# Splitting B22 alone, and T1 and t2 as one operation, in the 7-product steps of a transformer block

## The chip, the cores and the metric

The kernel runs on one core of a Trainium2 chip. The metric is the device time of one execution in microseconds (us); the time before is the median of three runs. A core has five engines with a queue of instructions each: TensorE (PE, with its weight loads shown apart as PEld), VectorE (DVE), ScalarE (ACT), GpSimd (POOL) and SyncE (SP). Each works through its queue in order; semaphores make one wait for another.

## The reference

One layer of a residual block on x of 256 tokens by 4096 channels in float32. Cut to what matters here:

```python
h = rms_norm(x, pre_norm_gain)
proj = h @ w_in                       # 4096 x 24704, split into q, k, v, gates, ...
y_a = dsa_attention(q, k, v, ...) * silu(gate_a)
y_b = ssd_mixer(xs, z, bm, cm, ...)
merged = sigmoid(g0) * (y_a @ w_branch_attn) + sigmoid(g1) * (y_b @ w_branch_ssd)
x = x + rms_norm(merged @ w_out, post_norm_gain)
```

Nearly all the work is in products of a 256-row activation with large float32 weights.

## The kernel before

**Number format.** Every float32 operand is split into a high half h (rounded by a copy to TensorE's fp32r format on ScalarE) and a low half l (operand minus h, on VectorE). A product is three matmuls: al·bh, ah·bl, ah·bh, each 128x128 by 128x512.

**Pairs.** A pair of 512-column blocks of a weight matrix is one call of `pair_gemm`. It runs over 16 (or 8) steps; a step has 256 rows of the weight, loaded by SP as two tiles, `ra` (B12 and B22) and `rb` (B11 and B21), two steps ahead. The four 128x512 blocks meet four 128x128 blocks of the activation. A step of kind "S" uses a Strassen-Winograd scheme of 7 products (21 matmuls), one of kind "D" or "R" the plain 8 products (24 matmuls). There are 226 S steps. The list of S steps in a pair is a tuple such as `SX` = (1, 3, 4, 6, 7, 9, 10, 12, 14); `SG`, used from the fourth of the eight gate pairs on, ends in 12, 13, 14 (in the last gate pair the steps from 8 on are plain). The activation's sums S1 to S4 are made beforehand (`ext`, against `b` for the plain blocks).

**An S step.** POOL issues a DMA that adds B11 onto B12 in `ra[:, 0]`, which makes T1's source. Then the weight's halves are made, for products in this order: with B21 (bank 2) and B11 (1), with B22 (3), with T1 (5), t2 (6), t3 (7) and t4 (4). In the code before: `rb` is split whole (1024 columns); B22 is copied to h (L636) and subtracted to l (L637); T1's source is copied to h (L638); t2 = T1 - B22 is formed in place over B22 (L641); t3 and t4 = `rb` - t2 are formed in place (L642, 1024 columns); T1's low half is made (L644, kept in this place by `keep_in_program_order`); t2 is split alone, then t3 and t4 together. L641 and L642 are called the block sums below.

**Tiles.** The halves lie in tiles `wh` and `wl` of 1024 columns from a ring of 4 each, and in one half tile (`wh1`, `wl1`, 512 columns, a single buffer), which t2 uses. A tile is free again when TensorE has done the last matmul that reads it.

**Order.** The order of each engine's instructions is set by a scheduler when the kernel is built. It walks the program by priority and takes what is ready by its own estimates, so that work of other parts (evictions of a pair's banks L563 to L590, the rotation of q and k L739 to L744, attention, the convolution L887) is put in between, and matmuls of a product can be moved by a place or two.

Of the kernel before, what the change touches and what calls it, by code (L numbers as in the profile page):

```python
# [13 lines left out]
AF = mybir.ActivationFunctionType  # L14
# [34 lines left out]
def fused_block(tc, x, xT, w_qi, w_misc, w_q0, w_qk, w_vg, w_x, w_z, w_gate, w_br, w_out2,  # L49
                percol, rows, tabs, tris, pgain, out):  # L50
    nc = tc.nc
    V, A, G, T = nc.vector, nc.scalar, nc.gpsimd, nc.tensor
# [21 lines left out]
    def fbit(ap):  # L74
        return ap.bitcast(F32)
# [427 lines left out]
    def split_tiles(n):  # L503
        if n == 1:
            return (whp.tile([P, 1, NW], F32R, tag="wh1", bufs=1, name="wh"),
                    wlp.tile([P, 1, NW], F32R, tag="wl1", bufs=1, name="wl"))
        return (whp.tile([P, n, NW], F32R, tag="wh", name="wh"),
                wlp.tile([P, n, NW], F32R, tag="wl", name="wl"))

    def split(src, n, sign=1, at=None):  # L510
        h, l = at() if at else split_tiles(n)
        A.activation(h, src, AF.Copy, scale=float(sign))  # L512
        if sign < 0:
            V.scalar_tensor_tensor(l, src, -1.0, fbit(h), ALU.mult, ALU.subtract)  # L514
        else:
            V.tensor_sub(l, src, fbit(h))  # L516
        return [(h[:, j, :], l[:, j, :]) for j in range(n)]
# [23 lines left out]
    def pair_gemm(what, mode, chunk, plan, outs, evac, hooks={}, pace=1, tail=0, spares=None, done=None):  # L541

        while len(live) > 1:
            drain(live.popleft())
        left = {}
        for _, kind in plan:
            for j, n in USES[kind].items():
                left[j] = left.get(j, 0) + n
        ps = {}
        dest = []  # L550

        def product(j, i, name, w):
            (ah, al), (bh, bl) = form(i, name), w
            first = j not in ps
            if first:
                ps[j] = bank(phys[j])
            left[j] -= 1
            for n, (l, r) in enumerate(((al, bh), (ah, bl), (ah, bh))):
                T.matmul(ps[j], l, r, start=first and n == 0, stop=left[j] == 0 and n == 2)  # L559

        def early():
            dest.extend(outs())
            A.activation(dest[0], ps[1], AF.Copy)  # L563
            V.tensor_add(dest[1], ps[6], dest[0])
            V.tensor_add(dest[2], ps[7], dest[1])

        def late():
            if not dest:
                dest.extend(outs())
                A.activation(dest[1], ps[5], AF.Copy, scale=-1.0)  # L570
                return
            V.tensor_add(dest[1], ps[5], dest[1])
            if 8 in ended:
                V.tensor_sub(dest[3], dest[3], ps[5])
                return
            V.scalar_tensor_tensor(dest[3], ps[5], -1.0, dest[2], ALU.mult, ALU.subtract)

        def rest():
            c11, c12, c21, c22 = dest
            if 1 not in ps:  # L580
                A.activation(c11, ps[2], AF.Copy)
                A.activation(c21, ps[4], AF.Copy)
                V.tensor_sub(c22, c12, ps[8])
                V.tensor_sub(c12, c12, ps[3])
                return
            V.scalar_tensor_tensor(c12, ps[3], -1.0, c12, ALU.mult, ALU.subtract)
            if 8 in ps and 8 not in ended:
                V.tensor_sub(c22, c22, ps[8])
            V.tensor_add(c11, ps[2], c11)
            V.tensor_add(c21, ps[4], c21)  # L590

        def end():
            rest()
            live.append(push(evac(dest)))

        def closing(tails):
            c11, c12, c21, c22 = dest
            V.scalar_tensor_tensor(c12, ps[3], -1.0, c12, ALU.mult, ALU.subtract)
            V.tensor_add(c11, ps[2], c11)
            done(0, dest)  # L600
            for j in (8, 4):
                for i, w in tails:
                    for k in (1, 2):
                        product(j, i, f"A2{k}", w[k, 2 if j == 8 else 1])
            V.tensor_sub(c22, c22, ps[8])
            V.tensor_add(c21, ps[4], c21)
            done(1, dest)

        tails = []
        after = max([n for n, (_, kind) in enumerate(plan) if kind == "S"], default=-2) + 1  # L610
        ended = []
        loaded = deque()

        def fetch(n):
            i, kind = plan[n]
            ra, rb = raw_tile(), raw_tile()
            load_half(ra, chunk(i), 0)
            load_half(rb, chunk(i), 1)
            if kind == "S":
                nc.gpsimd.dma_start(ra[:, 0, :], chunk(i)[:, HK, :], accum_op=ALU.add)  # L620
            loaded.append((ra, rb))

        for n in range(LEAD):
            fetch(n)
        for n, (i, kind) in enumerate(plan):
            if n + LEAD < len(plan):
                fetch(n + LEAD)
            ra, rb = loaded.popleft()
            if n in hooks:
                hooks[n]()  # L630
            assert kind_of[i] == what, (n, i, kind_of, len(aux))
            assert kind == "R" or ext_n[i] == {"S": 4, "D": 2}[kind], (n, i, ext_n)
            if kind == "S":
                b11, b21 = split(rb, 2)
                h, l = split_tiles(2)
                A.activation(h[:, 1, :], ra[:, 1, :], AF.Copy)  # L636
                V.tensor_sub(l[:, 1, :], ra[:, 1, :], fbit(h[:, 1, :]))  # L637
                A.activation(h[:, 0, :], ra[:, 0, :], AF.Copy)  # L638
                if n == 1:
                    run_pending()  # L640
                V.tensor_sub(ra[:, 1, :], ra[:, 0, :], ra[:, 1, :])  # L641
                V.tensor_sub(rb, rb, ra[:, 1:2, :].to_broadcast([P, 2, NW]))  # L642
                tc.keep_in_program_order(
                    V.tensor_sub(l[:, 0, :], ra[:, 0, :], fbit(h[:, 0, :])))  # L644
                t1, b22 = ((h[:, j, :], l[:, j, :]) for j in range(2))
                t2, = split(ra[:, 1:2, :], 1)
                t3, t4 = split(rb, 2)
                now = {1: ("A11", b11), 2: ("A12", b21), 3: ("S4", b22), 4: ("A22", t4),
                       5: ("S1", t1), 6: ("S2", t2), 7: ("S3", t3)}
                for j in (2, 1, 3, 5, 6, 7, 4):  # L650
                    product(j, i, *now[j])
            else:
                w = {}
                at = spares if n == len(plan) - tail + 1 else None
                w[1, 2], w[2, 2] = split(ra, 2, -1, at)
                w[1, 1], w[2, 1] = split(rb, 2, 1, at)
                if n == 0 and len(pending) > 1 and turned[0] == "aux":
                    pending.pop(0)()
                if n == 1:
                    run_pending()  # L660
                if n >= len(plan) - tail:
                    assert kind == "R" and dest
                    tails.append((i, w))
                    for k, j in ((1, 3), (2, 3), (1, 2), (2, 2)):
                        product(j, i, f"A1{k}", w[k, 1 if j == 2 else 2])
                    step(2 * pace)
                    continue
                if n == after:
                    early()
                    if not left.get(5):  # L670
                        late()
                        ended.append(5)
                if n == len(plan) - 1 and dest and not ended and left.get(8) == 0:
                    V.scalar_tensor_tensor(dest[3], dest[2], -1.0, ps[8], ALU.mult, ALU.subtract)
                    ended.append(8)
                todo = [(k, j) for j in ((5, 3, 2, 4) if kind == "D" else (3, 8, 2, 4))
                        for k in (1, 2)]
                for k, j in todo:
                    name = {2: f"A1{k}", 4: f"A2{k}", 8: f"A2{k}", 5: f"A2{k}",
                            3: f"D{k}" if kind == "D" else f"A1{k}"}[j]  # L680
                    product(j, i, name, w[k, 1 if j in (2, 4) else 2])
                    if (k, j) == todo[3]:
                        step(pace)
            step(pace)
        if tail:
            closing(tails)
            return
        if 5 not in ended:
            pending.append(late)
        pending.append(end)  # L690
        turn(mode)
# [733 lines left out]
```

## Time and profile before

| what | value |
|---|---|
| time, median of 3 runs (lowest, highest) | 2805.91 us (2803.67, 2806.32) |
| profiled execution | 2806.09 us |
| its span, first to last instruction | 2804.2 us |
| mean granted TensorE clock | 0.998 |
| PE / DVE / ACT / POOL busy | 99% / 90% / 65% / 8% |
| DMA | 651.75 MB, mean 232 GB/s |

The page gives the busy time of each engine, then 40 slices of the span, the DMA queues, the chain of waits that ended last, and groups of instructions by line. On the chain, 93% of the span is PE and 4% DVE. A row of a group reads: line, engine, operation, written tile <- read tiles, shapes and count, then busy us and mean ns of one, then the engine's idle time just before them and what ended it. A row of the timeline reads: start, duration, engine, line, operation, tiles, count of merged instructions, and in brackets the idle time before it and what ended it.

### The profile page before, as it was taken

The page shows a single profiled execution, that of the slowest core. Times are in us where ns is not written, and L with a number is a line of the kernel's source. Part 1 is how long each engine was busy: PE and PEld are TensorE (multiplying, and loading weights), DVE is VectorE, ACT ScalarE, POOL GpSimd, SP SyncE. Part 2 cuts the span into 40 slices and gives each one's busy share as a digit, 9 for nine tenths or more (in the row PEclk, how much of TensorE's full clock was granted, in tenths as well). Part 3 has the DMA queues.
Part 4 walks back from the last instruction along what each step waited for, and adds up shares of the span by engine and source line. Part 5 has one row for each costly group of instructions (what it writes and reads, how often), then busy time and mean ns, then how long its engine had stood idle before and what let it go on. Part 6 is the DMA issues. An engine that isn't in the chain of part 4 may idle for free.

```text
span 2804.2 us, 36892 instructions
## 1 busy us (share of the span) xinstructions
PE 2780.0 (99%) x12598; PEld 2282.7 (81%) x12598; DVE 2536.2 (90%) x3352; ACT 1815.1 (65%) x2564; POOL 226.6 (8%) x271
## 2 busy tenths in 40 slices
PE   9999999999999999999999999999999999999998
PEld 7877888888888888787888788888888888788886
DVE  7668999999999988989898999999987999988998
ACT  7444566665666666887788866666665656656664
POOL 0100000000000000000000010111010100000000
PEclk9999999999999999999999999999999999999999
DMA  9544777777777777576767788888877788867886
GB/s 379 194 165 143 221 222 230 236 211 221 232 227 229 220 220 233 173 226 200 220 190 217 224 255 255 254 253 251 262 260 246 249 274 265 276 223 234 241 253 214
DMA packets 205326, 651.75 MB, mean 232 GB/s; under 512 B 23120, under 2 KB 23888, under 8 KB 205136
## 3 DMA queue, kind: packets, MB, share of 16 engines
q1 hardware_dynamic: 161424, 566.52, 60.1%
q0 software_dynamic: 34784, 66.60, 13.5%
q10 hardware_dynamic: 8928, 16.26, 1.5%
q8 instruction: 99, 1.62, 0.2%
q14 instruction: 91, 0.75, 0.1%
HBM read 629.37 MB, written 19.92 MB: 232 GB/s over the span
## 4 chain that ended last, share of the span: by engine, by line
PE 93%; DVE 4%; ACT 1%; issue 1%; DMA 1%; DVEq 0%; SPq 0%; ACTq 0%
PE p L559 80%; PE p L211 3%; PE p L212 3%; PE p L213 3%; PE p L382 1%; DVE wl L516 1%; ACT wh L512 0%; PE p L413 0%; PE p L951 0%; DVE raw L642 0%; PE p L816 0%; PE p L783 0%; DVE cacc L887 0%; DVE raw L641 0%; ACT L889 0%
## 5 line engine op out<-in xcount | busy, mean ns | idle before, releaser
L559 PE MATMUL p<-wh,b 128*128 128x512 f32 x4536 | 1490.3, 393 | 0.4 <-ACT wh L512 0.2
L512 ACT ACTIVATE wh<-raw 128x1024 fp32r<-128x1024 f32 (+1 forms) x1154 | 1093.8, 972 | 612.3 <-DVE raw L641 262.5
L516 DVE TENSOR_TENSOR wl<-raw,wh 128x1024 fp32r<-128x1024 f32 (+1 forms) x916 | 983.0, 1089 | 70.6 <-ACT wh L512 61.9
L559 PEld LDWEIGHTS p<-wh,b 128*128 128x128 f32 x4536 | 851.7, 188 | 177.5 <-ACT wh L512 2.9
L559 PE MATMUL p<-wl,b 128*128 128x512 f32 x2268 | 884.9, 390 | 1.3 <-DVE wl L514 1.3
L559 PE MATMUL p<-wh,ext 128*128 128x512 f32 x2436 | 816.2, 390 | 1.5 <-ACT wh L512 1.0
L559 PEld LDWEIGHTS p<-wh,ext 128*128 128x128 f32 x2436 | 457.8, 188 | 96.5 <-ACT wh L512 2.7
L559 PEld LDWEIGHTS p<-wl,b 128*128 128x128 f32 x2268 | 426.4, 188 | 87.6 <-DVE wl L514 1.8
L559 PE MATMUL p<-wl,ext 128*128 128x512 f32 x1218 | 480.5, 394 | 3.7 <-DVE wl L644 3.4
L514 DVE SCALAR_TENSOR_TENSOR wl<-raw,wh 128x1024 fp32r<-128x1024 f32 x238 | 290.1, 1219 | 45.7 <-ACT wh L512 45.0
L642 DVE TENSOR_TENSOR raw<-raw 128x1024 f32<-128x1024 f32 x226 | 276.5, 1223 | 5.9
L559 PEld LDWEIGHTS p<-wl,ext 128*128 128x128 f32 x1218 | 228.9, 188 | 64.6 <-DVE wl L644 11.2
L636 ACT ACTIVATE wh<-raw 128x512 fp32r<-128x512 f32 x226 | 142.2, 629 | 115.8 <-PE p L559 105.5
L637 DVE TENSOR_TENSOR wl<-raw,wh 128x512 fp32r<-128x512 f32 x226 | 155.1, 686 | 19.1 <-ACT wh L636 17.3
L641 DVE TENSOR_TENSOR raw<-raw 128x512 f32<-128x512 f32 x226 | 155.7, 689 | 5.1
L644 DVE TENSOR_TENSOR wl<-raw,wh 128x512 fp32r<-128x512 f32 x226 | 154.5, 684 | 0.0
L211 PE MATMUL p<-wh,b 128*128 128x512 f32 x384 | 152.0, 397 | 1.1 <-DVE b L282 0.8
L212 PE MATMUL p<-wl,b 128*128 128x512 f32 x384 | 150.3, 392 | 0.0
L213 PE MATMUL p<-wh,b 128*128 128x512 f32 x384 | 150.2, 391 | 0.0
L203 DVE TENSOR_TENSOR wl<-raw,wh 128x1024 fp32r<-128x1024 f32 x80 | 100.6, 1259 | 47.8 <-ACT wh L202 47.7
L202 ACT ACTIVATE wh<-raw 128x1024 fp32r<-128x1024 f32 x80 | 84.5, 1058 | 88.6 <-PE p L213 76.6
L638 ACT ACTIVATE wh<-raw 128x512 fp32r<-128x512 f32 x226 | 139.4, 617 | 3.2 <-ACT yraw L386 3.2
(253 smaller groups left out, 1782.4 us busy)
## 6 DMA issues: line engine op xcount, KB each, us to landing
raw<-w_gate_d SPq DMA_DIRECT2D x256, 512.0 KB, 5.6
raw<-w_vg_d SPq DMA_DIRECT2D x128, 512.0 KB, 5.2
raw<-w_x_d SPq DMA_DIRECT2D x128, 512.0 KB, 5.2
raw<-w_br_d SPq DMA_DIRECT2D x128, 512.0 KB, 5.3
raw<-w_out_d SPq DMA_DIRECT2D x128, 512.0 KB, 5.3
raw<-w_qk_d SPq DMA_DIRECT2D x96, 512.0 KB, 5.0
raw<-w_z_d SPq DMA_DIRECT2D x64, 512.0 KB, 5.3
raw<-w_qi_d SPq DMA_DIRECT2D x62, 512.0 KB, 7.0
```

The costliest lines, as they stand in the source:

```text
L211: T.matmul(ps[t], al[:, tk], wh[:, i, :], start=first, stop=False)
L212: T.matmul(ps[t], ah[:, tk], wl[:, i, :], start=False, stop=False)
L213: T.matmul(ps[t], ah[:, tk], wh[:, i, :], start=False, stop=last)
L512: A.activation(h, src, AF.Copy, scale=float(sign))
L514: V.scalar_tensor_tensor(l, src, -1.0, fbit(h), ALU.mult, ALU.subtract)
L516: V.tensor_sub(l, src, fbit(h))
L559: T.matmul(ps[j], l, r, start=first and n == 0, stop=left[j] == 0 and n == 2)
L636: A.activation(h[:, 1, :], ra[:, 1, :], AF.Copy)
L637: V.tensor_sub(l[:, 1, :], ra[:, 1, :], fbit(h[:, 1, :]))
L641: V.tensor_sub(ra[:, 1, :], ra[:, 0, :], ra[:, 1, :])
L642: V.tensor_sub(rb, rb, ra[:, 1:2, :].to_broadcast([P, 2, NW]))
L644: V.tensor_sub(l[:, 0, :], ra[:, 0, :], fbit(h[:, 0, :])))
```

## The change

B22 is split alone and in the half tile (copy and subtraction by the helper `split`, so their lines are L512 and L516). T1 is no longer split ahead of the block sums: T1 and t2 lie side by side in `ra` once the first block sum has run, and are split together as one operation of 1024 columns behind the block sums. ScalarE and VectorE each lose one instruction per S step. The forced place of T1's low half goes too. Lines behind the edit move up by 6; the block sums become L638 and L639, the rotation L733 to L738.

```diff
             if kind == "S":
                 b11, b21 = split(rb, 2)
-                h, l = split_tiles(2)
-                A.activation(h[:, 1, :], ra[:, 1, :], AF.Copy)
-                V.tensor_sub(l[:, 1, :], ra[:, 1, :], fbit(h[:, 1, :]))
-                A.activation(h[:, 0, :], ra[:, 0, :], AF.Copy)
+                b22, = split(ra[:, 1:2, :], 1)
                 if n == 1:
                     run_pending()
                 V.tensor_sub(ra[:, 1, :], ra[:, 0, :], ra[:, 1, :])
                 V.tensor_sub(rb, rb, ra[:, 1:2, :].to_broadcast([P, 2, NW]))
-                tc.keep_in_program_order(
-                    V.tensor_sub(l[:, 0, :], ra[:, 0, :], fbit(h[:, 0, :])))
-                t1, b22 = ((h[:, j, :], l[:, j, :]) for j in range(2))
-                t2, = split(ra[:, 1:2, :], 1)
+                t1, t2 = split(ra, 2)
                 t3, t4 = split(rb, 2)
```

The engines' queues shift with it. First VectorE in the last S step of the fourth gate pair (step 14, the third S step in a row). The numbers behind names tell buffers apart; raw_15969 is `ra` and raw_15970 `rb`. Before:

```order
L516 TENSOR_TENSOR wl_16061<-raw_15970,wh_16060 128x1024
L637 TENSOR_TENSOR wl_16065<-raw_15969,wh_16064 128x512
L641 TENSOR_TENSOR raw_15969<-raw_15969 128x512
L642 TENSOR_TENSOR raw_15970<-raw_15970,raw_15969 128x1024
L644 TENSOR_TENSOR wl_16065<-raw_15969,wh_16064 128x512
L516 TENSOR_TENSOR wl_16073<-raw_15969,wh_16072 128x512
L516 TENSOR_TENSOR wl_16077<-raw_15970,wh_16076 128x1024
```

The same step on VectorE after the change, where raw_15695 is `ra` and raw_15696 `rb`:

```order
L516 TENSOR_TENSOR wl_15783<-raw_15696,wh_15782 128x1024
L516 TENSOR_TENSOR wl_15787<-raw_15695,wh_15786 128x512
L638 TENSOR_TENSOR raw_15695<-raw_15695 128x512
L639 TENSOR_TENSOR raw_15696<-raw_15696,raw_15695 128x1024
L516 TENSOR_TENSOR wl_15793<-raw_15695,wh_15792 128x1024
L516 TENSOR_TENSOR wl_15797<-raw_15696,wh_15796 128x1024
```

Behind the block sums one operation of 1024 columns stands in the place of L644 and the short L516; the rest keeps its place. TensorE in the same step, from T1's product (bank p3) over t2's (p4) to t3's (p8) and t4's (p1). Before:

```order
L559 MATMUL p3_15525<-wh_16064,ext_3115 128x512
L559 MATMUL p3_15525<-wl_16065,ext_3115 128x512
L559 MATMUL p3_15525<-wh_16064,ext_3115 128x512
L559 MATMUL p4_15529<-wh_16072,ext_3115 128x512
L559 MATMUL p4_15529<-wl_16073,ext_3115 128x512
L559 MATMUL p4_15529<-wh_16072,ext_3115 128x512
L559 MATMUL p8_15533<-wh_16076,ext_3115 128x512
L559 MATMUL p1_15479<-wh_16076,b14_92 128x512
L559 MATMUL p8_15533<-wl_16077,ext_3115 128x512
```

And TensorE there after the change:

```order
L559 MATMUL p3_15263<-wh_15792,ext_3107 128x512
L559 MATMUL p4_15267<-wh_15792,ext_3107 128x512
L559 MATMUL p3_15263<-wl_15793,ext_3107 128x512
L559 MATMUL p3_15263<-wh_15792,ext_3107 128x512
L559 MATMUL p4_15267<-wl_15793,ext_3107 128x512
L559 MATMUL p4_15267<-wh_15792,ext_3107 128x512
L559 MATMUL p8_15271<-wh_15796,ext_3107 128x512
L559 MATMUL p1_15219<-wh_15796,b14_92 128x512
L559 MATMUL p8_15271<-wl_15797,ext_3107 128x512
```

The first matmul of t2's product has moved ahead of the one that needs T1's low half. ScalarE there has the copies for T1 with t2 and for t3 with t4 (wh_15792, wh_15796) after the change, with one eviction in between:

```order
L512 ACTIVATE wh_15782<-raw_15696 128x1024
L512 ACTIVATE wh_15786<-raw_15695 128x512
L512 ACTIVATE wh_15792<-raw_15695 128x1024
L563 ACTIVATE pc_15829<-p7_15256 128x512
L512 ACTIVATE wh_15796<-raw_15696 128x1024
```

Before, that eviction (L563) stood behind the last copy of the step. The third place is VectorE in a q/k pair of the attention part, where the rotation of the pair before (tiles pc and m2, L739 to L744) is done between the splits; it is the S step whose T1 TensorE takes at 514.65 us. Before:

```order
L516 TENSOR_TENSOR wl_4656<-raw_4564,wh_4655 128x1024
L637 TENSOR_TENSOR wl_4660<-raw_4563,wh_4659 128x512
L744 TENSOR_TENSOR pc_4291<-pc_4291,m2_4740 128x512
L641 TENSOR_TENSOR raw_4563<-raw_4563 128x512
L739 TENSOR_TENSOR m2_4924<-pc_4292,tab_129 128x4x64
L642 TENSOR_TENSOR raw_4564<-raw_4564,raw_4563 128x1024
L644 TENSOR_TENSOR wl_4660<-raw_4563,wh_4659 128x512
L516 TENSOR_TENSOR wl_4668<-raw_4563,wh_4667 128x512
L516 TENSOR_TENSOR wl_4672<-raw_4564,wh_4671 128x1024
```

The same step after the change, where pc_4256 is the fourth and last tile to be rotated (before: pc_4292):

```order
L516 TENSOR_TENSOR wl_4612<-raw_4522,wh_4611 128x1024
L516 TENSOR_TENSOR wl_4616<-raw_4521,wh_4615 128x512
L737 TENSOR_TENSOR pc_4256<-pc_4256,m2_4872 128x512
L638 TENSOR_TENSOR raw_4521<-raw_4521 128x512
L738 TENSOR_TENSOR pc_4256<-pc_4256,m2_4872 128x512
L639 TENSOR_TENSOR raw_4522<-raw_4522,raw_4521 128x1024
L516 TENSOR_TENSOR wl_4622<-raw_4521,wh_4621 128x1024
L516 TENSOR_TENSOR wl_4708<-raw_4606,wh_4707 128x512
L516 TENSOR_TENSOR wl_4626<-raw_4522,wh_4625 128x1024
```

Here the rotation ends within this step, three operations further than before (one of 256 columns, two of 512), and B22 of the next S step (raw_4606) is split ahead of t3 and t4. In some other S steps the new order runs B22's split up to a step earlier, and the split of T1 with t2 ahead of the second block sum.

## Prediction

> **What bounds the kernel now.** I read the page first, then the waits of TensorE's weight loads, then the groups of instructions by shape, then the timeline of two places.
>
> ```profile
> span 2804.2 us, 36892 instructions
> PE 2780.0 (99%) x12598; PEld 2282.7 (81%) x12598; DVE 2536.2 (90%) x3352; ACT 1815.1 (65%) x2564; POOL 226.6 (8%) x271
> PEclk9999999999999999999999999999999999999999
> ```
>
> TensorE is busy 99% of the span at the full granted clock. The edit takes no matmul away, so it can only move the moments at which TensorE waits. Who makes it wait stands in the waits of its weight loads (us in total, times, longest):
>
> ```profile
> PEld p L559 <- DVE wl L644: 11.2, 22, 1.2
> PEld p L559 <- DVE wl L516: 7.0, 26, 0.4
> PEld p L559 <- ACT wh L512: 5.7, 18, 1.2
> PEld p L559 <- DVE wl L514: 1.8, 1, 1.8
> ```
>
> That is 25.7 us, 0.9% of the span, and it bounds any gain. The largest line is L644, T1's low half, which the edit rewrites; L516 holds t2, t3/t4 and other splits. VectorE is the late engine: 90% busy over the span, and full where it matters (below).
>
> **What the edit removes and adds.** The groups, with their means:
>
> ```profile
> L516 DVE TENSOR_TENSOR wl<-raw,wh 128x1024 fp32r<-128x1024 f32 x690 | 835.1, 1221 | 69.9 <-ACT wh L512 61.3
> L516 DVE TENSOR_TENSOR wl<-raw,wh 128x512 fp32r<-128x512 f32 x226 | 154.6, 684 | 0.6 <-ACT wh L512 0.6
> L644 DVE TENSOR_TENSOR wl<-raw,wh 128x512 fp32r<-128x512 f32 x226 | 154.5, 684 | 0.0
> L512 ACT ACTIVATE wh<-raw 128x1024 fp32r<-128x1024 f32 x928 | 951.6, 1055 | 349.6 <-PE p L559 203.3 <-DVE raw L642 131.6 <-ACT pc L1067 1.9
> L638 ACT ACTIVATE wh<-raw 128x512 fp32r<-128x512 f32 x226 | 139.4, 617 | 3.2 <-ACT yraw L386 3.2
> ```
>
> There are 226 seven-product steps. In each, VectorE trades two subtractions of 512 (L644 and the short L516) for one of 1024, and ScalarE two copies of 512 for one. By the means that is 2 x 0.684 - 1.221 = 0.147 us on VectorE and about 0.19 us on ScalarE. But successive instructions overlap. The timeline shows what they occupy, in the middle and the last of three 7-product steps in a row at the end of a gate pair (the row of 1772.05 begins the middle step; that of 1776.38 holds its t2, its t3/t4 and the first split of the last):
>
> ```profile
> 1772.05 1.23 DVE L516 TENSOR_TENSOR wl<-raw,wh 128x1024 fp32r<-128x1024 f32 x1 [0.37 <-ACT wh L512]
> 1773.19 0.68 DVE L637 TENSOR_TENSOR wl<-raw,wh 128x512 fp32r<-128x512 f32 x1
> 1776.38 2.97 DVE L516 TENSOR_TENSOR wl<-raw,wh 128x512 fp32r<-128x512 f32 x3
> 1779.99 0.69 DVE L641 TENSOR_TENSOR raw<-raw 128x512 f32<-128x512 f32 x1
> 1780.71 1.23 DVE L642 TENSOR_TENSOR raw<-raw 128x1024 f32<-128x1024 f32 x1
> 1781.86 0.68 DVE L644 TENSOR_TENSOR wl<-raw,wh 128x512 fp32r<-128x512 f32 x1
> 1782.46 1.83 DVE L516 TENSOR_TENSOR wl<-raw,wh 128x512 fp32r<-128x512 f32 x2
> ```
>
> A 512 occupies 1782.46 - 1781.86 = 0.60 us and a 1024 occupies 1781.86 - 1780.71 = 1.15, so the merge frees 0.05 to 0.06 us, 226 x 0.06 = 13.6 us in all. The Trainium skill, Perfetto Trace Analysis, "Optimizing Scalar/DVE Operations", gives about 60 ns of overhead for a VectorE operation on SBUF; the row agrees, and the sum by the page would also be 13.6 us. The same section also says that where these engines are not saturated but cause bubbles on others, breaking instructions up may let work finish sooner. That rule speaks against this edit, which joins two; it is the first rival.
>
> **How much of the saving reaches TensorE.** In a step with nothing in between, hardly any. t3/t4's low half needs ScalarE's copy, and that one waits for L642:
>
> ```profile
> 1772.31 0.63 ACT L636 ACTIVATE wh<-raw 128x512 fp32r<-128x512 f32 x1 [0.30 <-PE p L559]
> 1781.97 2.96 ACT L512 ACTIVATE wh<-raw 128x1024 fp32r<-128x1024 f32 x3 [0.54 <-DVE raw L642]
> 1784.84 0.58 ACT L563 ACTIVATE pc<-p 128x512 f32<-128x512 f32 x1
> ```
>
> The copy starts 1.26 us after L642 and is ready near 1783.03. L516 for t3/t4 starts at 1782.46 + 1.83 - 1.22 = 1783.07; behind a merged operation it could start at 1781.86 + 1.15 = 1783.01 but still waits for the copy. There the saving is 0 to 0.06 us. Where other VectorE work stands in the gap the full 0.06 comes through and a gap of about 0.07 closes too. The 48 waits on VectorE (22 + 26) fall on about 35 steps, an estimate since the two lines often follow each other; with two 7-product steps since VectorE last idled, 35 x 2 x 0.06 = 4.2 us. Ends: 0, and 13.6. I take **-4.2**, near the low end, because most of the 13.6 lies where TensorE waits for nothing. ScalarE's saving I cost at nothing: it is 65% busy, and its copies wait for L641, L642 or free tiles (349.6 us of idle before L512). Its cover gone would show as more than the 5.7 us above.
>
> **T1 comes later.** T1's low half is ready 1.22 instead of 0.68 us after its start, 0.54 later; t2's is 0.06 earlier (0.60 + 0.68 = 1.28 against 1.22). L641, L642 and t3/t4 stay. TensorE's new order, shown ahead of this for one place, puts t2's first matmul ahead of T1's low one, which hides one matmul, 0.23 us by the spacing in the rows of the next part. That leaves 0.31 us if nothing later binds, and 0.04 if the wait for t3/t4 that follows was binding anyway (7.0 us over 26 is 0.27 each). Of 22 waits for L644, four belong to the triples and six to the rotations below; 12 x 0.15 = **+1.8**, half way since the two lines have about equal counts. Ends: 0.5 (12 x 0.04) and 6.8 (22 x 0.31, which also allows for near misses that no view of waits shows).
>
> **The triples.** A gate pair from the fourth on (four of them by the plan in the code) ends in steps 12, 13, 14, all with seven products. TensorE there, first to last (x2 is two matmuls):
>
> ```profile
> 1772.52 0.62 PE L559 MATMUL p<-wh,ext 128*128 128x512 f32 x2
> 1777.73 0.39 PE L559 MATMUL p<-wl,ext 128*128 128x512 f32 x1
> 1782.60 0.50 PE L559 MATMUL p<-wl,ext 128*128 128x512 f32 x1
> 1782.94 0.64 PE L559 MATMUL p<-wh,ext 128*128 128x512 f32 x2
> 1783.41 0.39 PE L559 MATMUL p<-wl,ext 128*128 128x512 f32 x1
> 1784.35 0.50 PE L559 MATMUL p<-wl,ext 128*128 128x512 f32 x1
> ```
>
> Now B22 uses the single half tile, which is free once the third product of the 7-product step before is done: for the middle step that is the first matmul of the row at 1772.52, over at 1772.91. L636 began at 1772.31. So B22's copy ends near 1773.58 (0.63 later, and a little for the signal) and its low half starts at 1773.63 instead of 1773.19, 0.44 late. Behind it on ScalarE stand only copies that need VectorE's later results; on VectorE everything waits. The middle step bears it: T1's low half began 0.60 before 1776.38; the merged one would end at 1775.78 + 0.44 + 1.22 = 1777.44, before TensorE takes it at 1777.73. VectorE runs on without a gap, so the third step starts 0.44 late too. Its merged low half is ready at 1781.86 + 0.44 + 1.22 = 1783.52 and TensorE starts on it at 1783.57 instead of 1782.60. Six matmuls later (0.34 for the one behind a wait, as from 1782.60 to 1782.94, then 0.23 each, as from there to 1783.41 with two) comes t3's low one, at 1785.05 instead of 1784.35. Its operand is there: L563 now stands between two copies on ScalarE, so t3/t4's copy ends near 1783.71 (1781.2 when L641 is done, 0.95 for the merged copy, the spacing in the row of three, 0.5 for L563, 1.06 for its own) and its low half at 1784.97. So 0.70 us each, 4 x 0.70 = **+2.8**; ends 0.8 (no delay by the half tile) and 4.4.
>
> **The rotations.** In three q/k pairs the previous pair is rotated on VectorE while this one runs, and VectorE is full:
>
> ```profile
> 484.00:535.00 51.00, 50.95 (x65) 1.00 0.75 220
> 512.44 0.41 DVE L739 TENSOR_TENSOR m<-pc,tab 128x256 f32<-128x256 f32 x1
> 512.77 1.22 DVE L642 TENSOR_TENSOR raw<-raw 128x1024 f32<-128x1024 f32 x1
> 513.91 0.68 DVE L644 TENSOR_TENSOR wl<-raw,wh 128x512 fp32r<-128x512 f32 x1
> 514.65 0.50 PE L559 MATMUL p<-wl,ext 128*128 128x512 f32 x1
> ```
>
> The new order has three rotation operations more ahead of this T1: one of 256 columns (512.77 - 512.44 = 0.33) and two of 512 (0.60 each), 1.53 us, less about 0.4 saved by three merges and closed gaps. The merged half would be ready at 514.59 + 0.54 + 1.53 - 0.4 = 516.26: TensorE, which took T1 at 514.65, waits up to 1.65 longer. The same operations are then missing from the next steps, and VectorE's work over these 51 us shrinks a little, so some comes back. Ends 0 and 1.65 per pair; 1.0 is nearer the upper, since a wait once suffered is not refunded. 3 x 1.0 = **+3.0**.
>
> B22 hoisted ahead of the evictions between pairs delays these by 0.60 us; I cost that at nothing, since VectorE works a step ahead there and B22 would have followed anyway. If that cover is gone, L514 or L564 is what is late next. Transfers keep their order but for one neighbouring pair on POOL's queue and five small loads (saved gates, a gain, a residual) on SP's, which move past one to three neighbours; weights are fetched two steps ahead, which covers both, and SP's and POOL's waits would show it if not.
>
> Sum: -4.2 + 1.8 + 2.8 + 3.0 = +3.4 us. On the profiled execution's 2806.09 (its span plus 1.9 outside) that gives **2809.5**; the median of the runs, 2805.91, lies within 0.2 of it. That is +0.12%, within 0.2% (5.6 us), about what a measurement can tell.
>
> **Rivals.** (1) Slower: T1's lateness falls through in full. The place is every step with a wait for L644, the price 0.54 x 22 = 11.9, with the half tile's 4 x 0.44 = 1.8 and less the 4.2: +9.5, 2815.6. For it: L644 is the largest wait, and VectorE is full where it occurs. Against: t3/t4 binds in many of these steps. It decides once the mean loss of such a step passes 0.45 us (5.6 + 4.2 = 9.8 over 22). (2) Faster: VectorE's freed time is what the waits lack. If t3/t4 binds wherever T1 is late, lateness costs nothing, and the 7.0 us of L516 waits go: 2799.1. For it: VectorE 99.9% busy for 51 us. Against: the copy behind L642. (3) The edit doesn't do what it says: the order now splits B22 up to a step ahead and runs the merged operation before L642 in some steps, so that T1 is not late there; the 1.8 falls away and the triples keep only 0.8: -4.2 + 0.8 + 3.0, about 2805.7. Against: the triples and rotations keep the block sums first.
>
> **How the numbers follow.** Forecast 0.53 (its own range 2804 to 2814; 0.12 of it beyond 2811.5), rival 1 0.20, rival 2 0.14, rival 3 0.13 (0.02 of it below 2800.3). So slower by over 0.2% 0.12 + 0.20 = 0.32, faster 0.14 + 0.02 = 0.16, within 0.52. The range 2799 to 2818 runs from rival 2 past rival 1 and leaves out some 0.2.
>
> **What would show it.** Right: 226 fewer instructions on VectorE and on ScalarE; waits of weight loads for L516 grown from 18.2 us (L644 and L516 together) to 20 to 26; near 1783 a wait of about 1 us for the merged half; idle of VectorE before B22's low half in second steps. Wrong: if those waits shrink, or if waits for L564 or PE's idle at the pair boundaries grow, a term that I set at nothing did it.

## The result, and the profile after

The changed kernel is slower: 2822.15 us (median of 6 runs, 2820.95 to 2822.72) against 2804.72 us (6 runs, 2803.05 to 2806.32). The ratio is 1.0062, 95% interval 1.0052 to 1.0073. The forecast was 2809.5 with a range up to 2818; the loss is some 17 us where 3.4 were forecast.

The page of the changed kernel: span, busy times, and the chain of work that ended last.

```profile
span 2820.8 us, 36663 instructions
PE 2785.6 (99%) x12598; PEld 2280.8 (81%) x12598; DVE 2523.7 (89%) x3126; ACT 1783.2 (63%) x2336; POOL 226.7 (8%) x271
PE 84%; DVE 9%; ACT 4%; issue 3%; DMA 1%; DVEq 0%; ACTq 0%; SPq 0%
```

VectorE lost 226 instructions and 12.5 us of busy time (2536.2 before), 0.055 us per step; ScalarE lost 228 instructions and 31.9 us. Both savings came. But VectorE's and ScalarE's shares of the chain have grown from 4% and 1% to 9% and 4%. The waits of the weight loads say where (us in total, times, longest):

```profile
PEld p L559 <- DVE wl L516: 19.6, 38, 1.2
PEld p L559 <- ACT wh L512: 18.4, 31, 1.3
PEld p L559 <- DVE wl L514: 1.8, 3, 1.3
PEld p L559 <- DVE pc L564: 1.5, 2, 1.0
```

Waits for VectorE's low halves hardly grew (L644 and L516 together were 18.2). Waits for ScalarE's copy, L512, grew from 5.7 to 18.4. That is the engine at 63%, whose part in the change the prediction had costed at nothing.

To find the places I set the k-th L559 matmul of one trace against the k-th of the other and noted how much the distance grows from stretch to stretch. This is worked out from both traces and is no view of the profile; where a stretch is cut moves a single place by up to 0.25 us:

| places (times of before) | growth, us |
|---|---|
| six places in gate and later pairs (1809.9, 1891.9, 1973.9, 2050.5, 2266.7, 2350.7) | 6 x 1.14 = 6.8 |
| rotations (510.6, 684.5, 858.5) | 1.16 + 0.86 + 0.87 = 2.9 |
| triples (1782, 1858.8, 1940.9, 2022.9) | 0.59 + 0.85 + 0.73 + 0.73 = 2.9 |
| first pair with 7-product steps (310) | 2.6 |
| attention, a softmax operation ahead of the joined split (410, 578, 752, 926) | 4 x 0.55 = 2.2 |
| all the rest, gains and losses, as remainder | -0.8 |
| change of span | 16.6 |

The remainder holds two things of the one profiled execution of before, which make the change of span look smaller: its granted clock was 0.79 from 1545 to 1553 (1.00 at the same place after), which cost it some 1.7 us, and TensorE waited 1.75 us at 2103 for one low half of L514.

Triples and rotations came as forecast (2.8 and 3.0). The largest row was in no term. The timeline of VectorE and ScalarE at one of its places, 1809.9 in time of before, and TensorE's rows with a wait:

```profile
1821.55 4.43 ACT L512 ACTIVATE wh<-raw 128x512 fp32r<-128x512 f32 x5 [1.27 <-PE p L559]
1822.22 0.69 DVE L516 TENSOR_TENSOR wl<-raw,wh 128x512 fp32r<-128x512 f32 x1 [0.63 <-ACT wh L512]
1823.17 1.23 DVE L516 TENSOR_TENSOR wl<-raw,wh 128x1024 fp32r<-128x1024 f32 x1 [0.26 <-ACT wh L512]
1823.18 0.50 PE L559 MATMUL p<-wh,ext 128*128 128x512 f32 x1 [0.33 <-ACT wh L512]
1824.13 0.73 PE L559 MATMUL p<-wh,b 128*128 128x512 f32 x2 [0.21 <-ACT wh L512]
```

The first of the five copies (128x512) is B22 of the *next* 7-product step. ScalarE stood still for 1.27 us before it, until TensorE was done with the half tile, which holds B22 of the step in progress. The second copy, behind it in the queue, is t3/t4 of the step in progress, and TensorE waits for exactly that one at 1823.18. ScalarE's order there (steps 142 and 143 of the 226; raw_15967 and raw_15968 are `ra` and `rb` of the one, raw_16051 and raw_16052 of the other) has the two the other way round from before:

```
L512 ACTIVATE wh_16066<-raw_15967 128x1024   T1 and t2, this step
L512 ACTIVATE wh_16140<-raw_16051 128x512    B22, next step
L512 ACTIVATE wh_16070<-raw_15968 128x1024   t3 and t4, this step
```

Before, the copy of t3/t4 (the first of the four below) started 0.03 us after L642 was done, and TensorE took the same matmul (1814.64) without a wait:

```profile
1812.44 3.91 ACT L512 ACTIVATE wh<-raw 128x1024 fp32r<-128x1024 f32 x4 [0.54 <-DVE raw L642]
1814.64 0.39 PE L559 MATMUL p<-wh,ext 128*128 128x512 f32 x1
```

In the whole order B22's copy stands ahead of the previous step's t3/t4 in 11 steps on ScalarE (23, 41, 59, 87, 108, 143, 153, 163, 172, 184, 192), and its subtraction so on VectorE in 8 of them. Before, it does so in none of these. Six of the eleven are the six places of the table (143, 153, 163, 172, 184, 192). At five of them the copy waits 1.27 to 1.58 us for TensorE to free the half tile; at the sixth (172, 2050.5 in time of before) ScalarE idles only 0.21 us, and 0.7 of the 1.14 is a wait for the joined low half. At the other five the half tile is free by then, and the copy waits for nothing.

The first pair loses its 2.6 us in another way, and the prediction had no term for it either. VectorE's order has the first step's B22 and its first block sum well ahead of the pair, and that sum waits for the transfer into `ra`. TensorE pays some 20 us later (timeline and waits of VectorE after):

```profile
294.72 0.69 DVE L638 TENSOR_TENSOR raw<-raw 128x512 f32<-128x512 f32 x1 [2.99 <-DMA raw<-w_vg_d]
315.89 0.50 PE L559 MATMUL p<-wl,ext 128*128 128x512 f32 x1 [0.80 <-DVE wl L516]
318.43 0.50 PE L559 MATMUL p<-wl,b 128*128 128x512 f32 x1 [0.86 <-DVE wl L514]
DVE raw L638 <- DMA raw<-w_vg_d: 3.0, 1, 3.0
```

Before, no row of VectorE's waits names a transfer. Three later sums wait for one too (1.8 to 6.3 us), and TensorE loses under 0.3 us there.

At the triples the wait is where the prediction put it, near 1783 in time of before (timeline after):

```profile
1780.98 0.69 DVE L516 TENSOR_TENSOR wl<-raw,wh 128x512 fp32r<-128x512 f32 x1 [0.31 <-ACT wh L512]
1789.70 0.30 PEld L559 LDWEIGHTS p<-wh,ext 128*128 128x128 f32 x2 [0.34 <-ACT wh L512]
1791.00 0.19 PEld L559 LDWEIGHTS p<-wl,ext 128*128 128x128 f32 x1 [1.00 <-DVE wl L516]
1792.38 0.19 PEld L559 LDWEIGHTS p<-wl,ext 128*128 128x128 f32 x1 [0.15 <-DVE wl L516]
```

VectorE idles 0.31 ahead of the middle step's B22, and TensorE waits 1.00 for the joined low half of the third step. At the first rotation the size was right (timeline after):

```profile
517.83 1.23 DVE L639 TENSOR_TENSOR raw<-raw 128x1024 f32<-128x1024 f32 x1
518.97 2.97 DVE L516 TENSOR_TENSOR wl<-raw,wh 128x1024 fp32r<-128x1024 f32 x3
520.20 0.19 PEld L559 LDWEIGHTS p<-wh,ext 128*128 128x128 f32 x1 [1.25 <-ACT wh L512]
```

The joined low half is ready at 518.97 + 1.22 = 520.19. TensorE's wait of 1.25 ends at 520.20 too, but on ScalarE's copy of t3 and t4: the order has put a matmul with t3/t4's high half ahead of T1's low one, and that copy cannot start before L639 is done at 519.06. Both are late by the rotation operations ahead of the block sums.

### The profile page after: what moved, and what is told of

It reads as the page before. It is cut to its first block, busy times and chain, and to the rows that moved or that the text cites. A ratio compares the mean times of both kernels' runs of the same rounds, so it can differ in the third digit from the quotient of the medians.

```text
span 2820.8 us, 36663 instructions
## 1 busy us (share of the span) xinstructions
PE 2785.6 (99%) x12598; PEld 2280.8 (81%) x12598; DVE 2523.7 (89%) x3126; ACT 1783.2 (63%) x2336; POOL 226.7 (8%) x271
## 4 chain that ended last, share of the span: by engine, by line
PE 84%; DVE 9%; ACT 4%; issue 3%; DMA 1%; DVEq 0%; ACTq 0%; SPq 0%
PE p L559 73%; DVE wl L516 3%; PE p L211 2%; PE p L212 2%; PE p L213 2%; ACT wh L512 2%; DVE raw L639 1%; DVE raw L638 1%; DVE wl L203 1%; PE p L382 1%; PE p L413 0%; DVE cacc L881 0%; PE p L945 0%; PE p L810 0%; PE p L777 0%
## 5 line engine op out<-in xcount | busy, mean ns | idle before, releaser
L512 ACT ACTIVATE wh<-raw 128x1024 fp32r<-128x1024 f32 (+1 forms) x1380 | 1318.1, 985 | 753.9 <-DVE raw L638 323.0
L559 PE MATMUL p<-wh,b 128*128 128x512 f32 x4536 | 1489.2, 393 | 1.7 <-ACT wh L512 1.6
L516 DVE TENSOR_TENSOR wl<-raw,wh 128x1024 fp32r<-128x1024 f32 (+1 forms) x1142 | 1251.7, 1116 | 121.9 <-ACT wh L512 107.4
L559 PEld LDWEIGHTS p<-wh,b 128*128 128x128 f32 x4536 | 851.0, 188 | 178.8 <-ACT wh L512 6.3
L559 PE MATMUL p<-wl,b 128*128 128x512 f32 x2268 | 886.0, 391 | 1.0 <-DVE wl L514 0.9
L559 PE MATMUL p<-wh,ext 128*128 128x512 f32 x2436 | 820.6, 391 | 6.0 <-ACT wh L512 5.3
L559 PEld LDWEIGHTS p<-wh,ext 128*128 128x128 f32 x2436 | 456.4, 188 | 106.1 <-ACT wh L512 12.0
L559 PEld LDWEIGHTS p<-wl,b 128*128 128x128 f32 x2268 | 426.3, 188 | 89.5 <-DVE wl L514 1.8
L559 PE MATMUL p<-wl,ext 128*128 128x512 f32 x1218 | 478.1, 393 | 6.9 <-DVE wl L516 6.8
L514 DVE SCALAR_TENSOR_TENSOR wl<-raw,wh 128x1024 fp32r<-128x1024 f32 x238 | 290.4, 1221 | 30.8 <-ACT wh L512 30.8
L559 PEld LDWEIGHTS p<-wl,ext 128*128 128x128 f32 x1218 | 228.6, 188 | 65.9 <-DVE wl L516 17.9
L639 DVE TENSOR_TENSOR raw<-raw 128x1024 f32<-128x1024 f32 x226 | 276.4, 1223 | 4.8
L638 DVE TENSOR_TENSOR raw<-raw 128x512 f32<-128x512 f32 x226 | 156.0, 690 | 21.3 <-DMA raw<-w_out_d 6.9
L620 POOL DMA_DIRECT2D raw<-w_gate_d x66 | 57.2, 866 | 571.0 <-DMA raw<-w_gate_d 212.2
L211 PEld LDWEIGHTS p<-wh,b 128*128 128x128 f32 x384 | 71.9, 188 | 20.5 <-issue 2.6
L212 PEld LDWEIGHTS p<-wl,b 128*128 128x128 f32 x384 | 72.2, 188 | 15.7 <-DVE wl L200 1.0
L213 PEld LDWEIGHTS p<-wh,b 128*128 128x128 f32 x384 | 72.1, 188 | 15.8
```

Of the source, the lines that this page charges most:

```text
L211: T.matmul(ps[t], al[:, tk], wh[:, i, :], start=first, stop=False)
L212: T.matmul(ps[t], ah[:, tk], wl[:, i, :], start=False, stop=False)
L213: T.matmul(ps[t], ah[:, tk], wh[:, i, :], start=False, stop=last)
```

## The experiments

Two theories at the start. H, the hoist: with B22 in a single buffer, its copy taken up a step ahead blocks ScalarE's queue; that is about half of the loss, and T1's lateness with the triples is the rest. The rival: the half tile or the joined operation costs by itself, wherever B22 stands. All times below are medians against the kernel before, which stood at 2804.1 to 2804.5 in each set.

**B22 pinned.** The changed kernel, with B22's two instructions kept behind the split of B11 and B21 of their own step:

```diff
-                b22, = split(ra[:, 1:2, :], 1)
+                h, l = split_tiles(1)
+                tc.keep_in_program_order(A.activation(h, ra[:, 1:2, :], AF.Copy))
+                tc.keep_in_program_order(V.tensor_sub(l, ra[:, 1:2, :], fbit(h)))
+                b22 = h[:, 0, :], l[:, 0, :]
```

> The changed kernel with B22's copy and subtraction pinned behind the split of B11 and B21 of the same step on ScalarE and VectorE, so that no B22 stands ahead of the t3/t4 split of the step before (8 places do in the changed kernel: the rotations and the gate and branch pairs). Theory H (the hoisted B22 waits for the single half tile and t3/t4 wait behind it, 8 x 1.1 us): about 9 us come back, near 2813 us. Rival L (the lateness of T1 costs it in every step): nothing comes back, 2820 to 2824 us.

Measured 2813.97 (ratio 1.0034, 1.0021 to 1.0046): 8.2 us back. Its waits of weight loads:

```profile
PEld p L559 <- DVE wl L516: 18.8, 40, 1.6
PEld p L559 <- ACT wh L512: 12.9, 28, 0.9
```

Five of the six places are gone from the comparison of the traces and the sixth (2050.5) keeps 0.7, so 6.1 us of the waits for the half tile are undone. The 2.6 at the first pair and the 2.2 in the attention part are gone too, and no sum waits for a transfer any more; the four triples stay (0.64, 0.85, 0.71, 0.72), and the rotations keep 0.78, 0.52 and 0.51. The pin also holds B22 back in steps where it was early without harm, and takes back some 2.5 us of gain near 1550. So the 8.2 is the net worth of the whole free order. The expectation of 9 us came close, but not as it was worked out (eight places of 1.1): that is in part luck.

**The half tile without the joined operation.** T1 and t2 are split apart again, with T1 early:

```diff
                 b22, = split(ra[:, 1:2, :], 1)
+                h, l = split_tiles(2)
+                A.activation(h[:, 0, :], ra[:, 0, :], AF.Copy)
...
-                t1, t2 = split(ra, 2)
+                tc.keep_in_program_order(
+                    V.tensor_sub(l[:, 0, :], ra[:, 0, :], fbit(h[:, 0, :])))
+                A.activation(h[:, 1, :], ra[:, 1, :], AF.Copy)
+                V.tensor_sub(l[:, 1, :], ra[:, 1, :], fbit(h[:, 1, :]))
+                t1, t2 = ((h[:, j, :], l[:, j, :]) for j in range(2))
```

> B22 alone in the half tile as in the change, but T1 and t2 split as two operations of 512 columns each, T1 ahead of the block sums and its low half pinned right behind them, as before; as many instructions as before. Theory H: without a hoist ahead of t3/t4 the half tile costs the triples alone, 4 x 0.44: 2804 to 2809 us. Rival L: the same, since T1 is early. Rival C (the half tile costs everywhere that a 7-product step follows another): 2815 us or more.

Measured 2814.21 (ratio 1.0040, 1.0027 to 1.0054), a miss. The expectation held that the hoist belongs to the joined operation. It does not: in this order B22's copy stands ahead of the previous t3/t4 on ScalarE in 7 steps (87, 94, 108, 143, 153, 163, 172), though on VectorE in none. The same place in its timeline:

```profile
1817.15 4.43 ACT L512 ACTIVATE wh<-raw 128x512 fp32r<-128x512 f32 x5 [1.37 <-PE p L559]
1818.76 1.23 DVE L516 TENSOR_TENSOR wl<-raw,wh 128x1024 fp32r<-128x1024 f32 x1 [1.18 <-ACT wh L512]
1818.78 0.50 PE L559 MATMUL p<-wh,ext 128*128 128x512 f32 x1 [0.81 <-ACT wh L512]
```

ScalarE stands 1.37 us for the half tile, and VectorE 1.18 and TensorE 0.81 for t3/t4 behind it; the comparison gives +1.13 here, as with VectorE's hoist on top. So ScalarE's queue alone carries this cost. It does so at four places (4.6 us in all); the first pair loses 2.4 here too, and there the first sum (L640) again waits for its transfer, 2.55 us. By itself the run could not tell the half tile from the hoist; the run without hoist and without joining, below, did.

**The joined operation without the half tile.** B22 takes a tile of the ring:

```diff
-                b22, = split(ra[:, 1:2, :], 1)
+                h, l = split_tiles(2)
+                A.activation(h[:, 0, :], ra[:, 1, :], AF.Copy)
+                V.tensor_sub(l[:, 0, :], ra[:, 1, :], fbit(h[:, 0, :]))
+                b22 = h[:, 0, :], l[:, 0, :]
```

> T1 and t2 as one operation behind the block sums, as in the change, but B22 in a tile of the ring, not in the half tile; its order has no B22 ahead of the step before's t3/t4. The ring then serves four tiles in a 7-product step instead of three. Theory H: the merge alone costs T1's lateness, 5 to 9 us: 2810 to 2814 us. Rival L: 2818 us or more. Rival M (fewer and larger operations help once the half tile is out of the way): at or under 2804 us. A ring short of tiles would show as more waits of ScalarE for TensorE, and void the reading.

Measured 2856.44 (ratio 1.0185, 1.0171 to 1.0199). The waits of ScalarE for a free tile and of TensorE for its copy:

```profile
ACT wh L512 <- PE p L559: 374.6, 353, 3.5
PEld p L559 <- ACT wh L512: 58.0, 89, 1.4
```

A step needs four tiles instead of three and a half, and the ring runs short (the first row is 276.1 us in the changed kernel); the run says nothing on the question. A second buffer for the half tile would have been the clean test; it does not fit in the on-chip memory beside the other tiles, so it was not tried.

**Pinned, and the joined split taken early.** The pinned kernel with the joined split given high priority, so that in fewer steps other work of VectorE stands between it and the block sums.

```diff
-                t1, t2 = split(ra, 2)
+                with tc.high_priority():
+                    t1, t2 = split(ra, 2)
```

> The kernel of the first run with T1's and t2's merged split at high priority in the scheduler, so that less other work stands between the block sums and it (13 steps instead of 32). Theory H plus lateness: 2 to 4 us under the first run, since waits like the 0.64 us ones of the attention part (four, where a softmax operation stands ahead of the merged split) go. Rival: other work moved out of the gap comes back ahead of the block sums of the next step and the time is that of the first run within 1 us.

Measured 2815.8 (ratio 1.0040, 1.0028 to 1.0053), 1.8 above the pinned kernel: neither the theory nor the rival. With less work between the sums and the joined split the loss did not shrink, so nothing here speaks for that work as its cause; the order changed elsewhere too.

**Half tile, no joining, no hoist.** The second experiment's code with the pins of the first: B22 stays behind the split of B11 and B21 (the text below says sums).

> B22 alone in the half tile with its copy and its subtraction pinned behind the sums of its own step, T1 and t2 apart again and T1 early as in the kernel before: neither the merged operation nor the hoist ahead of t3/t4. Theory H (the hoist behind the single half tile costs some 1.1 us at each of six places, the rest of the loss is T1's lateness): only the triples keep 0.3 to 0.4 us each from the half tile, 2804 to 2807, and the waits for ScalarE's copy fall from 12.5 us (hoist free) to under 8. Rival: B22 in the single half tile costs by itself, wherever it is issued: about 2814, as without the pins.

Measured 2806.87 (ratio 1.0007, 0.9998 to 1.0016). H holds: without hoist and joining the times do not tell the half tile's cost from zero. Its waits (L646 is T1's low half):

```profile
PEld p L559 <- DVE wl L646: 10.7, 20, 1.2
PEld p L559 <- ACT wh L512: 7.2, 23, 0.7
PEld p L559 <- DVE wl L516: 4.2, 15, 0.5
PEld p L559 <- DVE wl L648: 1.9, 7, 0.3
PEld p L559 <- ACT wh L647: 0.8, 2, 0.4
```

With t2's halves, which have lines of their own here (L648, L647), that is 24.8 us against 23.9 before. The triples lose 0.32, 0.42, 0.31 and 0.32, 1.4 in all. Four runs now make a square (from three sets of runs, in which the kernel before stood at 2804.4 to 2804.7):

| us | B22 pinned | order free |
|---|---|---|
| T1 and t2 apart | 2806.9 | 2814.2 |
| T1 and t2 joined | 2814.0 | 2822.2 |

The free order of B22's split costs 7.3 or 8.2, joining 7.1 or 8.0, and the two add up within 1 us. Of the free order's cost, the waits for the half tile are 4.6 or 6.1 and the first pair's wait for its transfer 2.4 or 2.6, by the traces; other gains and losses of the two orders make up the difference.

**Half tile free one product earlier.** The pinned kernel with TensorE's products in the order B21, B22, B11, and the kernel before in that order as control (each `for j in (2, 1, 3, 5, 6, 7, 4)` becomes `(2, 3, 1, 5, 6, 7, 4)`).

> The changed kernel with B22 pinned (2814.0 in its own run), and TensorE's products in the order B21, B22, B11 instead of B21, B11, B22, so that the half tile is free one product (0.68 us) earlier. Theory: what is left of the loss there is mostly T1's lateness and only the triples' 0.4 us each is the half tile: 2812 to 2813. Rival: the half tile's late release sets the rest as well: under 2810.

> Control: the kernel before with the products in the order B21, B22, B11. The order of the products alone should move the time by less than 2 us either way, 2803 to 2807; what it moves is taken off the run of the pinned kernel in that order. Rival: B22's low half is taken 0.68 us earlier than VectorE has it, and the kernel is over 3 us slower.

Measured 2812.52 (ratio 1.0027, 1.0017 to 1.0037) and, for the control, 2805.2 (1.0002, 0.9993 to 1.0011). The pinned kernel gains some 1.5 us, or 2.2 with the control's 0.7 taken off. In the traces the triples lose 0.24 each instead of some 0.73, 2.0 us in all, a little more than their four times 0.3 to 0.4; the rest of its loss is not the half tile's release.

**A mixed form.** The form of before where the step ahead has seven products, the joined form with B22 pinned where it is a plain one:

```diff
+                if n and plan[n - 1][1] != "S":
...
                     t1, t2 = split(ra, 2)
+                else:
...
+                    t2, = split(ra[:, 1:2, :], 1)
```

> The form of the kernel before (B22 and T1 in one tile, T1 early, t2 alone) where the step ahead has seven products too, and the changed form with B22 pinned where the step ahead is a plain one. Theory (the loss is T1's lateness and the half tile in steps that follow one of seven products, where VectorE has no slack): 2802 to 2806, no loss at the triples, about 0.5 us each left at rotations if these steps are of the plain-ahead kind. Rival: the pinned kernel's remaining 9.5 us lies in steps behind plain ones, and it stays above 2810.

Measured 2811.26 (ratio 1.0024, 1.0015 to 1.0033), a miss. VectorE has 157 instructions less than before, so 157 of the 226 steps are joined. The triples lose 0.1 each and the rotations nothing, but 6.8 us stay, in the scan stage and the late pairs. Joining costs in steps behind plain ones too, where the expectation had seen no loss.

**Which engine's joining costs.** From the kernel with neither hoist nor joining (2806.9): once with ScalarE's copies joined alone, once with VectorE's subtractions joined alone.

```diff
-                A.activation(h[:, 0, :], ra[:, 0, :], AF.Copy)
...
-                A.activation(h[:, 1, :], ra[:, 1, :], AF.Copy)
+                A.activation(h, ra, AF.Copy)
```

> B22 alone in the half tile and pinned; of T1 and t2 only ScalarE's copies are joined (one of 1024 behind the sum that makes t2), VectorE's two subtractions stay apart with T1's first. So far: apart on both engines 2806.9, joined on both 2814.0. Theory V (the loss of joining is VectorE's: T1's low half comes 0.54 us later): 2806 to 2809. Theory A (it is ScalarE's: T1's copy, which could run ahead of the sums, now waits for t2's sum, and T1's low half and t3/t4's copy behind it): 2811 to 2814, with the waits for ScalarE's copy near 12.9 us instead of 7.2.

```diff
-                tc.keep_in_program_order(
-                    V.tensor_sub(l[:, 0, :], ra[:, 0, :], fbit(h[:, 0, :])))
...
-                V.tensor_sub(l[:, 1, :], ra[:, 1, :], fbit(h[:, 1, :]))
+                V.tensor_sub(l, ra, fbit(h))
```

> The other half: T1 and t2 copied apart on ScalarE, T1's copy ahead of the sums, and VectorE's subtractions joined to one of 1024. Theory V: 2812 to 2814, nearly the whole 7 us. Theory A: 2806 to 2809. If each half costs some 3 to 4 us, both are needed for the whole, and neither theory holds alone.

Copies alone: 2813.32 (ratio 1.0032, 1.0020 to 1.0044), +6.4. Subtractions alone: 2810.62 (ratio 1.0024, 1.0015 to 1.0033), +3.8. Neither theory holds alone. The two sum to more than the 7.1 of both: they overlap. They differ in place. Set against the trace of the kernel with neither, the joined subtraction loses 0.62, 0.51 and 0.56 at the rotations and 0.41, 0.42, 0.40 and 0.35 at the triples, 3.3 in all, which are the places of the forecast. The joined copy loses nothing above 0.4 there; it loses in the scan stage (1147 to 1570, some 3 us) and behind 2220 (some 3 more). Its waits (L644 is the joined copy, L646 and L647 the low halves of T1 and t2):

```profile
PEld p L559 <- DVE wl L646: 10.9, 24, 1.1
PEld p L559 <- ACT wh L512: 9.6, 30, 0.9
PEld p L559 <- DVE wl L516: 7.1, 23, 0.6
PEld p L559 <- ACT wh L644: 4.6, 9, 0.7
PEld p L559 <- DVE wl L647: 3.8, 13, 0.3
```

The row of L644 is new: TensorE waits for T1's *high* half. One place of it, timeline of the same kernel:

```profile
2357.56 0.69 DVE L641 TENSOR_TENSOR raw<-raw 128x512 f32<-128x512 f32 x1
2358.28 1.06 ACT L644 ACTIVATE wh<-raw 128x1024 fp32r<-128x1024 f32 x1 [2.29 <-DVE raw L641]
2359.40 0.73 PE L559 MATMUL p<-wh,ext 128*128 128x512 f32 x2 [0.24 <-ACT wh L644]
2360.16 0.19 PEld L559 LDWEIGHTS p<-wl,ext 128*128 128x128 f32 x1 [0.47 <-DVE wl L646]
```

ScalarE idles for 2.29 us before the copy, because the joined copy must wait for the sum L641 on VectorE. T1's copy apart needs no sum: in the kernel with the copies apart ScalarE makes it ahead, in what is idle time here. How much of the 6.4 is this wait, and how much the different order that the scheduler makes of it, the runs do not separate.

## Why the prediction was wrong, by its own steps

- **B22 hoisted, "I cost that at nothing, since VectorE works a step ahead there".** This is the step that failed first: the free order of B22's split costs 7.3 or 8.2 us. The sentence asked only for the evictions between pairs, and only for VectorE. Within the pairs a hoist ahead of t3/t4 had no term at all, and the queue that mattered was ScalarE's: the hoisted copy waits for the single half tile, and t3/t4's copy of the step in progress waits behind it (4.6 or 6.1 us). The prediction worked out the half tile's release for the triples to 0.1 us and did not ask what stands behind a copy that waits for it. One such hoist was on show ahead of it (raw_4606), at a place where the half tile is free in time. Ahead of the first pair the cover on VectorE was gone too: its queue stood 2.99 us for a transfer (2.6 us). The Trainium skill, PSUM — Partial Sum Buffer, "Engine vs sequencer instructions", says that ScalarE's and VectorE's queues are strictly first in, first out; the 1.27 us of idle ahead of five copies agrees.
- **"ScalarE's saving I cost at nothing: it is 65% busy".** A low share covered neither this nor the joined copy. It did name its own sign, the waits for L512, and that row rose from 5.7 to 18.4.
- **The saving, -4.2.** VectorE's freed 0.055 us per step came as worked out, 12.5 us in all. On TensorE's path it does not show: the subtractions joined alone free 15.0 us (2538.0 to 2523.0 busy) and lose 3.8.
- **T1 later elsewhere, +1.8.** Too small, and the wrong half. Joining costs 7.1; less the rotations (1.8) and the triples' growth (1.6), 3.7 is left where the prediction had -4.2 + 1.8 = -2.4. It shifted T1's low half by VectorE's longer operation alone and left out that T1's high half now waits for L638. How much of the 3.7 is that wait the runs leave open.
- **The triples, +2.8.** Right: 2.9 measured, and 1.4 of it the half tile alone against the 4 x 0.44 = 1.8 in the term.
- **The rotations, +3.0.** Right in size, 2.9, and in cause: operations of the rotation ahead of the sums. With B22 pinned 1.8 of it stays, so a part hung on the free order, which the term did not tell apart. The 1.0 for each was picked between 0 and 1.65, so that it fits so well is in part luck.
- **Transfers at nothing.** Wrong at the first pair. No row of TensorE's waits after names a transfer, but the sentence looked for trouble on SP's and POOL's queues alone. The new order has VectorE ask for T1's source earlier, and L638 waits for it there (2.99 us).
- **The rivals.** Rival 1 had the right sign, yet not its mechanism: its price was for T1's low half, whose joining alone costs 3.8. The rule of the Trainium skill behind it (Perfetto Trace Analysis, "Optimizing Scalar/DVE Operations": break instructions up where the engine makes others wait) held here: apart is 7.1 us faster than joined with B22 pinned. Rivals 2 and 3 fell; splitting B22 early, harmless in rival 3, was the largest loss.
- **The signs.** Those of being right nearly all came (226 instructions less, 1.00 us near 1783, VectorE's idle before B22; L516 at 19.6 where 20 to 26 was named), in a kernel that lost five times the forecast. They tested the terms of the sum and not what had no term.

## What to carry to other kernels

When an edit moves an operand into a single buffer, look in the new order for every instruction that writes that buffer, and ask what stands behind it in the same queue: the wait for the buffer is paid by those. The same goes for an instruction that moves ahead of the transfer that it needs. Count that on each engine that has a queue, however idle the engine is on average. And before joining two operations, ask for each input when it was ready alone: joining makes the earlier one wait for the later, on both engines that touch it, and 0.055 us of saved overhead does not pay for that where TensorE is 99% busy.

## What was not expected of the hardware

At five of the six places one copy of 0.63 us, which waits 1.27 to 1.58 us on an engine at 63%, cost TensorE some 1.15 us. At most 0.3 us of it came back over the next 40 us. With the half tile alone it was the same (1.13 to 1.17 at four places, ScalarE's idle 0.63 to 1.40): whether VectorE's queue was blocked as well (0.63 us of its idle at 1822.22 in the changed kernel) or only made to wait for t3/t4's copy (1.18 with the half tile alone) made no difference.
